# A weight-gradient matmul on one core: the accumulation order after slice 12 rearranged into whole phases, with the narrow part's banks taken in turn

## The chip, the cores and the metric

One core of one Trainium2 chip. The metric is the device time of the kernel in microseconds. The span of a profiled execution, from its first to its last instruction, is 1.7 to 1.9 us shorter than its measured time.

## The reference

```python
batch, m, k, n = 16, 512, 1024, 768
# float32 inputs
grad_weight = np.einsum('bmk,bmn->kn', input, grad_output)   # (1024, 768), float32
```

The 16 x 512 rows are one contraction of 8192, cut in 64 slices of 128.

## The kernel before: the parts that matter

The loads round each slice of both inputs to bfloat16 on the way in (all but slice 0, which is loaded as float32 and rounded by VectorE and ScalarE). They all stand at the start of the program, in order of slices, for GpSimd. In the trace GpSimd issues them one after the other, most of them when an earlier one has landed, the last at 136.8 us. There are 42 buffers for each input.

```python
for s in range(1, S):                       # S = 64
    gt = xg.tile([P, N], bf16, name="gt")   # grad_output, 128 x 768
    xt = xg.tile([P, K], bf16, name="xt")   # input, 128 x 1024
    nc.gpsimd.dma_start(out=gt, in_=G[s * P : (s + 1) * P, :])
    nc.gpsimd.dma_start(out=xt, in_=X[s * P : (s + 1) * P, :])
```

A slice needs twelve matmuls of 512 columns: four of part A and four of part B (output columns 0 to 511, wide) and four of the narrow part N (output columns 512 to 767, computed transposed). A part occupies four PSUM banks while it is open. There are eight banks and three parts, so the parts must take turns. When a part closes, VectorE adds its four banks to a sum in SBUF, and a bank can be reopened when its add is done.

```python
ORDER = (
    "A1! N1 B2! N2 A2 N3! A3 B3 A4! B5 N5 B6! N7 A6 N8! A9! B10 N9 B12! N12! A12! "
    "B15 A15 AB16 A19! B19! N19! A22 B22 AB28 A31! B31! N31! A34 B34 AB47 A50! B50! N64!"
).split()
# "A19!": run part A up to, not including, slice 19, then close it.
# "AB28": A and B by turns, slice by slice, up to slice 28.

def one_slice(part, close):
    s = part.done
    part.done += 1
    opened = part.banks is None
    if opened:                                # all four banks at once
        names = [free.pop(0) for _ in part.groups]
        part.banks = [(name, psum.tile([P, NA], f32, name=name)) for name in names]
    for i, (group, (name, bank)) in enumerate(zip(part.groups, part.banks)):
        part.matmul(bank, *group, s, opened, close)
        if close:
            ...                               # add (or first copy) to the sum in SBUF
            free.append(name)
    ...                                       # when it closes: the part has no banks any more
# ... afterwards: A and B from slice 50 on, bank by bank, each added and stored
```

## Time and profile before

| | before |
|---|---|
| median of the first three runs | 176.81 us (176.78 to 177.07) |
| span of the profiled run | 175.2 us |
| matmuls / weight loads in the program | 808 / 808 |
| VectorE instructions | 88 |
| x tile of one slice lands every | 2.2 us |
| TensorE needs for one slice (12 matmuls) | 2.59 us |

The lines that carry the reading are in the prediction below. How to read them: in a timeline each line is a start, a length, the engine, the source line, the operation and a count. A bracket at its end tells how long the engine had been idle and what ended that. L123 and L130 are the matmuls of the wide and the narrow parts, L114 is the adds. After the change the same lines are L124, L131 and L115. Matmuls are pipelined and the printed length of one (0.38 us) overlaps the next one's, so pace and pauses are read from starts. Some traces lack one matmul record in 50. Such a gap is one matmul of 0.216 us wide and is no pause.

### The profile page before, as it was taken

The numbers are of one execution on the slowest core, as the hardware profiler recorded it, in microseconds if no ns is written. First come the engines' busy times: TensorE is split into PE (matmuls) and PEld (weight loads), VectorE is DVE, ScalarE is ACT, GpSimd is POOL, SyncE is SP. The second block draws the span as 40 slices with busy tenths as digits, with TensorE's granted clock in tenths as the row PEclk, the third lists the DMA queues.
The fourth block names the chain that finished last, engine by engine and source line by source line (L and its number), as shares of the span: only waits on it lengthen the run. The fifth ranks groups of instructions, "written<-read, shape, count | busy, mean of one in ns | idle before, by whom it ended". The sixth has DMA issues, their size and how long they took to land.

```text
span 175.2 us, 1984 instructions
## 1 busy us (share of the span) xinstructions
PE 170.2 (97%) x793; PEld 78.3 (45%) x808; DVE 53.4 (30%) x88; ACT 5.7 (3%) x10; POOL 66.9 (38%) x130
## 2 busy tenths in 40 slices
PE   8999999999899999999999999999999999999993
PEld 3444444444344444444444444444444444444463
DVE  0555582880374100280320000047000003932122
ACT  3440000000000000000000000000000000000000
POOL 7544434444444444444444444444364200000000
PEclk9999999999999999999999999999999999999999
DMA  5999999999999999999999999999999990085623
GB/s 177 219 209 208 208 208 208 209 208 208 208 210 206 208 208 210 208 208 209 208 208 209 208 211 205 209 208 208 208 208 209 208 186 4 0 184 164 153 102 120
DMA packets 25192, 33.09 MB, mean 189 GB/s; under 512 B 6496, under 2 KB 16608, under 8 KB 25184
## 3 DMA queue, kind: packets, MB, share of 16 engines
q0 software_dynamic: 18144, 28.91, 90.3%
q1 hardware_dynamic: 2592, 2.49, 4.4%
q10 hardware_dynamic: 4448, 1.57, 3.9%
q8 instruction: 6, 0.10, 0.2%
q14 instruction: 2, 0.02, 0.0%
HBM read 58.72 MB, written 3.15 MB: 353 GB/s over the span
## 4 chain that ended last, share of the span: by engine, by line
PE 72%; DMA 24%; issue 1%; POOL 1%; DVE 0%; POOLq 0%
PE bank L123 46%; PE bank L130 26%; DMA xt<-in_input_dram 24%; POOL gt L92 1%; POOL xt L93 0%; DVE acc L114 0%; POOLq L228 0%
## 5 line engine op out<-in xcount | busy, mean ns | idle before, releaser
L123 PE MATMUL bank<-gt,xt 128*128 128x512 bf16 (+2 forms) x521 | 110.3, 368 | 1.2 <-DMA xt<-in_input_dram 0.6
L123 PEld LDWEIGHTS <-xt 128*128 128x128 bf16 x532 | 50.8, 98 | 59.2 <-DMA xt<-in_input_dram 1.4
L130 PE MATMUL bank<-xt,gt 128*128 128x512 bf16 x248 | 55.8, 379 | 0.2
L114 DVE TENSOR_TENSOR acc<-bank,acc 128x512 f32<-128x512 f32 (+2 forms) x54 | 33.1, 664 | 72.5 <-PE bank L123 71.9
L93 POOL DMA_DIRECT2D xt<-in_input_dram x63 | 33.5, 531 | 40.2 <-DMA xt<-in_input_dram 37.0
L92 POOL DMA_DIRECT2D gt<-in_grad_output_dram x63 | 33.5, 533 | 30.0 <-DMA gt<-in_grad_output_dram 28.5
L130 PEld LDWEIGHTS <-gt 128*128 128x128 bf16 x252 | 24.6, 98 | 29.8
L114 DVE TENSOR_TENSOR acct<-bank,acct 128x512 f32<-128x512 f32 x20 | 12.6, 679 | 39.4 <-PE bank L130 39.3
L80 PE MATMUL bank<-const-bfloat16-1.0 128*128 128x512 bf16 (+1 forms) x12 | 4.3, 547 | 0.8 <-PEq L228 0.8
L118 DVE COPY acc<-bank 128x512 f32<-128x512 f32 x4 | 2.7, 684 | 1.6 <-PE bank L123 1.5
L80 PEld LDWEIGHTS <-const-bfloat16-1.0 128*128 128x128 bf16 x12 | 1.6, 140 | 3.3 <-issue 3.3
L174 DVE STREAM_TRANSPOSE turned<-acct 128x512 f32<-128x512 f32 x4 | 2.9, 713 | 0.1
L123 PE MATMUL bank<-g,x 128*128 128x512 bf16 x8 | 2.7, 475 | 0.0
L120 ACT COPY acc<-bank 128x512 f32<-128x512 f32 x4 | 2.2, 587 | 1.8 <-PE bank L123 1.7
L105 DVE CAST g<-gf 128x256 bf16<-128x256 f32 x1 | 0.4, 440 | 4.2 <-DMA gf<-in_grad_output_dram 4.2
L118 DVE COPY acct<-bank 128x512 f32<-128x512 f32 x2 | 1.3, 686 | 1.3 <-PE bank L130 1.3
L106 ACT ACT_TABLE_LOAD x1 | 1.3, 1283 | 1.7 <-PEq L228 1.7
L123 PEld LDWEIGHTS <-x 128*128 128x128 bf16 x8 | 0.8, 114 | 1.1 <-issue 0.6
L120 ACT COPY acct<-bank 128x512 f32<-128x512 f32 x2 | 1.1, 588 | 1.5 <-PE bank L130 1.5
L130 PE MATMUL bank<-x,g 128*128 128x512 bf16 x4 | 1.0, 379 | 0.0
L106 ACT CAST x<-xf 128x256 bf16<-128x256 f32 x2 | 0.8, 402 | 0.5 <-DMA xf<-in_input_dram 0.5
L130 PEld LDWEIGHTS <-g 128*128 128x128 bf16 x4 | 0.4, 106 | 0.6 <-issue 0.3
(7 smaller groups left out, 1.7 us busy)
## 6 DMA issues: line engine op xcount, KB each, us to landing
xt<-in_input_dram POOLq DMA_DIRECT2D x63, 256.0 KB, 8.5
gt<-in_grad_output_dram POOLq DMA_DIRECT2D x63, 192.0 KB, 8.5
out_dram<-acc SPq DMA_DIRECT2D x13, 128.0 KB, 2.7
out_dram<-turned ACTq DMA_DIRECT2D x4, 256.0 KB, 3.2
xf<-in_input_dram ACTq DMA_DIRECT2D x2, 256.0 KB, 3.9
gf<-in_grad_output_dram SPq DMA_DIRECT2D x1, 256.0 KB, 3.5
out_dram<-acc SPq DMA_DIRECT2D x1, 256.0 KB, 2.0
gf<-in_grad_output_dram SPq DMA_DIRECT2D x1, 128.0 KB, 3.7
```

The lines of the kernel that those rows point to most:

```text
L80: nc.tensor.matmul(wps[:, 0:cols], ones, nc.const_aps.tensor(1.0, (P, cols), bf16), start=True, stop=True,)
L92: nc.gpsimd.dma_start(out=gt, in_=G[s * P : (s + 1) * P, :])
L93: nc.gpsimd.dma_start(out=xt, in_=X[s * P : (s + 1) * P, :])
L105: nc.vector.tensor_copy(out=dst[:, c : c + QX], in_=src[:, c : c + QX])
L106: nc.scalar.copy(out=dst[:, c + QX : c + 2 * QX], in_=src[:, c + QX : c + 2 * QX])
L114: nc.vector.tensor_add(out=dst, in0=src, in1=dst)
L118: nc.vector.tensor_copy(out=dst, in_=src)
L120: nc.scalar.copy(out=dst, in_=src)
L123: nc.tensor.matmul(bank, xs[s][:, k * P : (k + 1) * P], gwide[s][:, c0:c1], start=start, stop=stop)
L130: nc.tensor.matmul(bank, gnarrow[s].rearrange("p (r t) -> p t r", t=NT)[:, t], xs[s][:, h * NA : (h + 1) * NA], start=start, stop=stop,)
L174: nc.vector.transpose(out=turned[:, h * hb : (h + 1) * hb, :, t], in_=dst.rearrange("p (b r) -> p b r", r=SQ),)
```

## The change

Its intent: up to slice 12 nothing changes. After that A and B advance together through whole phases of 5, 9 and 15 slices, each followed by the narrow part over the same slices. The narrow part then takes its four banks one after the other (all slices of the phase into one bank, then the next), so that it needs a bank only when it comes to it. A small letter in the order stands for this.

```diff
-    "B15 A15 AB16 A19! B19! N19! A22 B22 AB28 A31! B31! N31! A34 B34 AB47 A50! B50! N64!"
+    "B15 AB17! n17! AB26! n26! AB41! n41! AB47 A50! B50! N64!"
...
+    def bank_by_bank(part, upto):
+        first = part.done
+        part.done = upto
+        for i in range(len(part.groups)):
+            open_bank(part, i)
+            for s in range(first, upto):
+                add_slice(part, i, s, s == first, s == upto - 1)
...
-        while any(parts[n].done < upto for n in names):
-            for n in names:
-                if parts[n].done < upto:
-                    one_slice(parts[n], close and parts[n].done == upto - 1)
+        if names.islower():
+            bank_by_bank(parts[names.upper()], upto)
+        else:
+            slice_by_slice(names, upto, close)
```

(The rest splits the old `one_slice` into `open_bank`, `add_slice` and `slice_by_slice`, which do for capital letters what it did.)

## The prediction

> **What bounds the kernel now.** I read the page first, then the list of waits, then the chain that ended last, and last the timelines of TensorE, VectorE and GpSimd around the one place where TensorE stood still. The page's first part and its strip of 40 slices:
>
> ```profile
> PE 170.2 (97%) x793; PEld 78.3 (45%) x808; DVE 53.4 (30%) x88; ACT 5.7 (3%) x10; POOL 66.9 (38%) x130
> ...
> PE   8999999999899999999999999999999999999993
> ...
> PEclk9999999999999999999999999999999999999999
> ```
>
> TensorE is busy from end to end at a full clock. The program has 808 matmuls (12 warm-up, 64 slices of 12, and 28 more because the last bank's 14 slices come in three pieces), and there are 808 weight loads but 793 matmul records: 15 are missing, so a busy share alone proves nothing. The pace has to come from starts. Timeline of TensorE, 20 to 56 us:
>
> ```profile
> 34.10 11.39 PE L123 MATMUL bank<-gt,xt 128*128 128x512 bf16 x51
> 46.07 3.63 PE L123 MATMUL bank<-gt,xt 128*128 128x512 bf16 x15 [0.58 <-DMA xt<-in_input_dram]
> 49.53 6.21 PE L130 MATMUL bank<-xt,gt 128*128 128x512 bf16 x28
> 55.58 0.59 PE L123 MATMUL bank<-gt,xt 128*128 128x512 bf16 x2
> ```
>
> The narrow part takes its slices 12 to 18 there, 7 x 4 = 28 matmuls, from 49.53 to 55.58: 6.05 / 28 = 0.216 us each. The stretch that begins at 34.10 holds 52 matmuls by the program (A of slices 9 to 11, B and A of 12 to 14, A and B of 15, A of 16 and 17; one record is missing). It should have ended at 34.10 + 52 x 0.216 = 45.33, and the next matmul, A of slice 18, started at 46.07. So TensorE really stood still 0.74 us (the 0.58 printed counts from a modelled end). The list of waits, its rows for TensorE and the weight loads that name a transfer or a bank:
>
> ```profile
> PEld L123 <- DMA xt<-in_input_dram: 1.4, 2, 1.1
> ...
> PE bank L123 <- DMA xt<-in_input_dram: 0.6, 1, 0.6
> ```
>
> No row has TensorE waiting for VectorE or ScalarE: banks are never late. The 1.1 is the weight load before this same matmul; the other weight-load gap, 0.3 us, moves no matmul start. The chain shows the same switch:
>
> ```profile
> 28.66 8.54 DMA xt<-in_input_dram
> 37.20 0.28 issue
> 37.48 8.54 DMA xt<-in_input_dram
> 46.02 0.05 issue
> 46.07 0.82 PE bank L123 x3
> ...
> 165.87 6.51 PE bank L123 x57
> 172.38 0.03 issue
> 172.40 0.29 DVE acc L114
> ```
>
> Up to 46 us the loads are on the chain, after it TensorE alone, with 0.05 us breaks that are the missing records. Slice 18's x tile landed at 46.02 and released its matmul 0.05 later. Slice 14's landed at 37.20, so a slice lands every (46.02 - 37.20) / 4 = 2.205 us, while TensorE needs 12 x 0.216 = 2.592 us for one. Loads are faster than TensorE, but the lead is small early on. The rest of the span is 4.91 us of start (first casts and warm-up) and about 3 us of the last add and store after the last matmul.
>
> **What the Trainium skill says.** "TensorE: Matmul & The Clock Gate", section "Wait — 56ns, not 53.3ns?", gives N / 2.4 GHz + about 2.5 ns between warm matmuls, 215.7 ns for 512 columns; the 0.216 us here agrees, so no order of matmuls can make one cheaper. "PSUM — Partial Sum Buffer", section "PSUM bank collisions raise a hardware error", wants a bank guarded against matmuls while another engine reads it; so a bank that is reopened must wait for its eviction, and each first matmul of a group in the changed order does wait on VectorE. "Perfetto Trace Analysis", section "Matmuls", wants independent groups to rotate through banks so that evictions overlap; both kernels do. "SBUF — State Buffer", section "Who interferes with whom", says that a VectorE instruction with at most one SBUF input outside the two-port modes does not contend with GpSimd, which matters because GpSimd makes the load descriptors. The adds read one bank and one SBUF tile. In this trace GpSimd issues x tiles at 46.31 and 48.52, during eight adds (46.50 to 51.57), and at 41.91 and 44.09 with VectorE idle: 2.21 against 2.18 us apart, so it agrees.
>
> **The change part by part.** The order up to slice 12, the start, the tail (A and B from slice 50, bank by bank) and all loads are untouched. Matmuls: the same 808, same shapes. Removed: the middle schedule, where A ran ahead to slice 18 alone. Added: A and B together to 17, narrow to 17; then to 26; then to 41; then as before. Closes of all three parts between 12 and 50/64 go from 9 to 12 groups of four, so 12 more adds.
>
> (a) *The 0.74 us wait.* Number the real matmuls from 0; slice 12 is complete at 144, B of 12 to 14 takes 144 to 155. A of slice 18 was number 184 at an unstalled 45.33. In the new order, "AB17" takes turns: A12, B15, A13, B16, A14, A15, A16. So B15 is number 160, at 45.33 - 24 x 0.216 = 40.15; its x tile landed at 46.02 - 3 x 2.205 = 39.41: 0.74 spare. B16 is number 168, at 41.87; slice 16 landed at 46.02 - 2 x 2.205 = 41.61: 0.26 spare, 0.21 after the 0.05 from landing to start. Number 184 is now the narrow part on slices 12 to 16, all there. No wait: **-0.74 us**.
>
> (b) *New waits for data?* The narrow part to 17 is 20 matmuls, so AB26 begins at 45.33 + 4.32 = 49.65. Each slice of AB takes 8 x 0.216 = 1.73 us against 2.205 between landings, so the lead shrinks by 0.48 a slice and is least at the last one. Slice 25: needed at 49.65 + 8 x 1.728 = 63.47, landed at 46.02 + 7 x 2.205 = 61.46, 2.0 spare. AB41 begins 108 matmuls after AB26, at 72.98; slice 40 is needed at 72.98 + 14 x 1.728 = 97.17 and lands at about 94.5, 2.6 spare. Slice 49 comes long after. The last: narrow on slice 63, number 652, at 45.33 + 468 x 0.216 = 146.42; by the last issue (136.8) plus 8.5 us to landing it lands at 145.3: 1.1 spare, where the kernel before had 1.84. **0**. The phases of 5, 9 and 15 look fitted to exactly these leads.
>
> (c) *New waits for banks?* An add starts 0.43 us after its group's last matmul starts (46.07 to 46.50), takes 0.69, and follows the next by about 0.60 (four in 2.48 us). Going into a narrow phase from slice 17 on, its first bank is the one A closed eight matmuls earlier: 8 x 0.216 - 0.43 - 0.69 = 0.61 us spare; into the first one it is B16's, closed long before. Within a phase a bank's turn lasts 5, 9 or 15 x 0.216 = 1.08, 1.94 or 3.24 us, longer than an add. Coming out, A takes banks evicted before, and B's fourth group takes the bank the narrow part closed last: 8 starts from that matmul to its reopening, again 0.61 spare. VectorE's queue must not be behind: in the shortest phase A's four adds run from 44.89, narrow adds follow at about 47.3, 47.9, 48.8 and 49.9, so the last is ready when its bank is. **0**.
>
> (d) *The 12 more adds*, 12 x 0.664 = 8.0 us by the row's mean, lie on an engine that is idle 70% of the span and end no wait. **0**.
>
> Sum: 176.81 - 0.74 = 176.07.
>
> **Rivals.** One: slice 16, with 0.2 us to spare, comes late. Landings slip in this very trace (slice 9's x tile landed 3.04 us after slice 8's). For it: a spare of 0.2 is smaller than such a slip. Against: a common lateness of all loads delays slice 11 first, which has no spare at all (B11 at 30.62 by the count, landed at 30.59), and so shifts TensorE as well. At worst it would take back what was gained: 176.3 to 176.8. Two: banks reopen late, because four narrow groups now close one by one among eight others. If all six phase edges lost 0.6 us by a slow release, 3.6 us would come to 179.7; the spare of 0.61 at each edge and the measured queue speak against. Three: consecutive matmuls into one bank run faster or slower than in rotation. The tail already does just that, at the same 10.79 us for 50, so 0 either way. Four: the extra adds hold up GpSimd and so loads; the issue distances above speak against it. Five: the tail or the stores hide the gain. TensorE alone is on the chain from 46 us to the last add, so 0.74 earlier there is 0.74 earlier at the end.
>
> **Range and chances.** The ceiling of the gain is the one wait, since nothing else on TensorE is idle: no less than about 176.0, with the run-to-run spread of 0.3 us below 175.8. Upward, rival one ends at 176.8. So 176.1, range 175.8 to 176.8. For 2% either way 3.5 us is needed: faster has nothing to come from (1 in 100), slower only by rival two or by something I don't see (2 in 100).
>
> **What would show it.** No gap in matmul starts at 45 to 47 us beyond one missing record; VectorE's count 100 in place of 88; narrow stretches of 20, 36 and 60 matmuls from about 45.3, 65.2 and 98.9 us; the last matmul 0.74 us earlier. Wrong if TensorE waits for slice 16 at 41.9, for slice 63 at 146, or if a wait for VectorE stands before a reopened bank.

## The result and the profile after

The changed kernel took 176.32 us (median of 4 runs, 176.06 to 176.42), the kernel before 176.89 us in the same set. The ratio is 0.9965, with a 95% interval of 0.9947 to 0.9982. A ratio here is the mean time of one kernel's fast runs over that of the other's of the same rounds, so it isn't quite the ratio of the medians quoted. Two more sets of runs gave 0.9954 and 0.9950 (below). So the gain is real and 0.35 to 0.5%, far under 2%.

The page of the changed kernel (busy time, share and count of each engine):

```profile
PE 170.8 (98%) x808; PEld 78.2 (45%) x808; DVE 60.8 (35%) x100; ACT 5.6 (3%) x10; POOL 66.9 (38%) x130
```

VectorE has 100 instructions where it had 88 and is busy 7.4 us longer. TensorE has the same work; this trace lost no record. The list of waits, limited to TensorE, has a single row, the one before the first warm-up matmul:

```profile
PE bank L81 <- PEq L252: 0.8, 1, 0.8
```

The row with 0.6 us for an x tile is gone. The timeline of TensorE shows the place itself:

```profile
34.20 11.39 PE L124 MATMUL bank<-gt,xt 128*128 128x512 bf16 x52
45.42 4.48 PE L131 MATMUL bank<-xt,gt 128*128 128x512 bf16 x20
49.74 15.70 PE L124 MATMUL bank<-gt,xt 128*128 128x512 bf16 x72
65.28 7.93 PE L131 MATMUL bank<-xt,gt 128*128 128x512 bf16 x36
```

The reader can check each start from the line above it: 34.20 + 52 x 0.216 = 45.43, then + 20 x 0.216 = 49.75, then + 72 x 0.216 = 65.3. There is no pause. The chain that ended last now runs without a load in it from 8.15 us to the end; its first and last pieces after that load are:

```profile
8.11 0.05 issue
8.15 1.04 PE bank L124 x4
...
147.46 24.26 PE bank L124 x140
171.71 0.02 issue
171.74 0.29 DVE acc L115
```

Before, the last add of the chain stood at 172.40; here at 171.74, 0.66 us earlier. That is the 0.74 us of the wait less about 0.1 us, and the 0.1 is seen in the first line of each timeline: the stretch that began at 34.10 before begins at 34.20 here, because slices 1 and 11 landed 0.24 and 0.10 us later in this execution. TensorE stood still 0.28 us for slice 1 and 0.12 us for slice 11 in this profile. Both are too short to be a row of that list. The order up to slice 12 is the same in both kernels, so slice 11 can hold up either of them: in the profile of the kernel before it cost 0.04 us. (The prediction has that this gap "moves no matmul start"; it moved them by those 0.04 us.)

The adds of the first new phase, in the timeline of VectorE:

```profile
42.38 5.08 DVE L115 TENSOR_TENSOR acc<-bank,acc 128x512 f32<-128x512 f32 x8 [3.56 <-PE bank L124]
47.37 1.28 DVE L115 TENSOR_TENSOR acct<-bank,acct 128x512 f32<-128x512 f32 x2
48.86 0.69 DVE L115 TENSOR_TENSOR acct<-bank,acct 128x512 f32<-128x512 f32 x1 [0.20 <-PE bank L131]
49.94 0.69 DVE L115 TENSOR_TENSOR acct<-bank,acct 128x512 f32<-128x512 f32 x1 [0.39 <-PE bank L131]
```

Four narrow banks end one by one, and their adds start at 47.37, 47.97 (the second of the x2), 48.86 and 49.94. The prediction had counted 47.3, 47.9, 48.8 and 49.9.

### The profile page after: what moved, and what is told of

Its sections match the earlier page's. It is cut to its first block, busy times and chain, and to the rows that moved or that the text cites. A ratio compares the mean times of both kernels' runs of the same rounds, so it can differ in the third digit from the quotient of the medians.

```text
span 174.5 us, 2024 instructions
## 1 busy us (share of the span) xinstructions
PE 170.8 (98%) x808; PEld 78.2 (45%) x808; DVE 60.8 (35%) x100; ACT 5.6 (3%) x10; POOL 66.9 (38%) x130
## 4 chain that ended last, share of the span: by engine, by line
PE 94%; DMA 4%; issue 0%; POOL 0%; DVE 0%; POOLq 0%
PE bank L124 63%; PE bank L131 31%; DMA xt<-in_input_dram 4%; POOL gt L93 0%; DVE acc L115 0%; POOLq L252 0%
## 5 line engine op out<-in xcount | busy, mean ns | idle before, releaser
L115 DVE TENSOR_TENSOR acc<-bank,acc 128x512 f32<-128x512 f32 (+2 forms) x62 | 37.9, 667 | 73.5 <-PE bank L124 73.1
L115 DVE TENSOR_TENSOR acct<-bank,acct 128x512 f32<-128x512 f32 x24 | 15.7, 682 | 30.0 <-PE bank L131 29.9
L106 DVE CAST x<-xf 128x256 bf16<-128x256 f32 x2 | 0.6, 287 | 0.3 <-DMA xf<-in_input_dram 0.3
```

What stands on the lines that cost most here:

```text
L106: nc.vector.tensor_copy(out=dst[:, c : c + QX], in_=src[:, c : c + QX])
L115: nc.vector.tensor_add(out=dst, in0=src, in1=dst)
```

## The experiments

The theory under test: the change removed one wait of 0.74 us for slice 18's data, and everything else in it costs and gains nothing. The rivals: whole phases or banks taken in turn make TensorE faster by themselves; the 12 more adds cost something; the small spares of the new schedule don't matter; and, the other way, the banks in turn don't matter either. There were seven runs of six kernels, in two sets with the kernel before in each (experiments 1 to 4 on one chip, 5 to 7 on another), and all gave correct results.

### 1. The change once more

No edit.

> The changed kernel once more, so that the others share a chip with it. Theory (the change removed one wait of 0.74 us for slice 18's data and cost nothing): 0.5 to 0.8 us under the kernel before of the same rounds. Rival (the difference on record was run-to-run spread, which is 0.3 us): anywhere from 0 to 0.3 us under it.

Measured: 176.12 us (5 runs), the kernel before 176.99 us (9 runs), ratio 0.9954, interval 0.9942 to 0.9967. By the medians 0.87 us, a little over the 0.5 to 0.8 expected. It isn't spread alone: no run of this set overlaps (176.30 is the slowest of one, 176.74 the fastest of the other).

### 2. Only the wait removed, in the old structure

```diff
-    "B15 A15 AB16 A19! B19! N19! A22 B22 AB28 A31! B31! N31! A34 B34 AB47 A50! B50! N64!"
+    "B15 A15 AB16 A18! B18! N18! A22 B22 AB28 A30! B30! N30! A34 B34 AB47 A50! B50! N64!"
```

> The kernel before, with its rotating narrow part, and only the two numbers changed that let A run ahead: to slices 18 and 30 in place of 19 and 31. Counted as in the prediction at 0.216 us a matmul: A of slice 18 is not needed until long after it landed, slice 29 just in time (under 0.1 us of wait), so TensorE loses 0.74 us less. Theory (the wait for data is all there is to the change): 0.6 to 0.75 us under the kernel before, level with the changed kernel within 0.2 us, with 88 VectorE instructions. Rival (taking narrow banks in turn or the whole phases make TensorE faster by themselves): near the kernel before, at least 0.3 us over the changed kernel. Second rival (the 12 more adds of the change cost something): under the changed kernel by more than 0.2 us.

Measured: 176.23 us, 0.76 us under the kernel before (0.6 to 0.75 expected), ratio to before 0.9963 (0.9950 to 0.9975), level with the changed kernel of the same set (0.9954) within 0.2 us. Its VectorE has 88 instructions. Its TensorE timeline:

```profile
34.27 13.11 PE L123 MATMUL bank<-gt,xt 128*128 128x512 bf16 x58
47.22 5.34 PE L130 MATMUL bank<-xt,gt 128*128 128x512 bf16 x24
```

By the order the first line holds 60 matmuls (A of 9 to 11, B and A of 12 to 14, A and B of 15, A of 16 and 17, B of 16 and 17; two records are missing), and 34.27 + 60 x 0.216 = 47.23. There is no pause. What follows: two changed numbers, without phases and without banks in turn, bring the whole gain. So neither of those makes TensorE faster, and the 12 adds that this kernel doesn't have cost the changed kernel nothing that these runs resolve. Slice 29, which the expectation had as just in time, had 0.28 us to spare (landed at 70.25, first used at 70.53). But TensorE lost 0.18 us for slice 49 (a gap of 0.393 us between starts in place of 0.216), which the expectation did not name. It is first used by matmul 504, at 45.33 + 320 x 0.216 = 114.45 by the count, and landed at 114.69 in this profile, which was taken of the slowest of the five runs (176.55): this order has no spare there. The changed one uses slice 49 only at 123.98, and it landed at 114.99. Since this kernel has a loss of its own, its time alone would not show a cost of the adds of up to 0.2 us; that they cost nothing is read from the changed kernel's timeline too, which has no pause after slice 11.

### 3. The wait put back, in the new structure

```diff
-    "B15 AB17! n17! AB26! n26! AB41! n41! AB47 A50! B50! N64!"
+    "B15 AB19! n19! AB26! n26! AB41! n41! AB47 A50! B50! N64!"
```

> The changed kernel with its first whole phase ending at slice 19 in place of 17. Theory: B of slice 17 is matmul 176, at 43.6 us, lands 43.8; B of slice 18 is matmul 184, lands 46.0; two waits of about 0.25 and 0.5 us, 0.74 in sum, so the time goes back to that of the kernel before (within 0.2 us) while the phases and the banks in turn stay. Rival (phases or banks in turn are what helped): stays within 0.3 us of the changed kernel.

Measured: 176.92 us, ratio to the kernel before 0.9997 (0.9985 to 1.0010). The timeline of TensorE:

```profile
34.08 11.67 PE L124 MATMUL bank<-gt,xt 128*128 128x512 bf16 x51
46.08 3.63 PE L124 MATMUL bank<-gt,xt 128*128 128x512 bf16 x15 [0.33 <-DMA xt<-in_input_dram]
49.55 6.21 PE L131 MATMUL bank<-xt,gt 128*128 128x512 bf16 x28
```

The stretch from 34.08 to slice 18 holds 52 matmuls, one record missing, and ends 0.77 us late: 46.08 - 34.08 - 52 x 0.216. By starts it is two gaps, 0.27 us for slice 17 and 0.50 us for slice 18; the first is hidden inside the line's 11.67, since the view joins what is less than 0.15 us apart by modelled ends. The narrow stretch then starts at 49.55, where the kernel before had 49.53. So the whole gain goes when the first phase is two slices longer, phases and banks in turn notwithstanding. That the wait alone decides, within the 0.2 us that these runs resolve, is shown from both sides.

### 4. The narrow part's banks all at once

```diff
-    "B15 AB17! n17! AB26! n26! AB41! n41! AB47 A50! B50! N64!"
+    "B15 AB17! N17! AB26! N26! AB41! N41! AB47 A50! B50! N64!"
```

> The changed kernel with the same phases, but the narrow part of phases 17, 26 and 41 again slice by slice over four banks at once. Theory (banks in turn are there because A and B now close together): the third and fourth bank of a part are reopened 10 and 11 matmuls after A0's last, 2.16 and 2.38 us, while their evictions end 0.43 + 2 or 3 x 0.60 + 0.69 = 2.3 and 2.9 us after it; about 0.24 and 0.38 us of wait at each of five phase edges, 3.1 us in sum, so about 179.4 us, and TensorE rows that wait for VectorE. Rival (VectorE's queue has room enough, banks in turn change nothing): within 0.3 us of the changed kernel and no wait for VectorE.

Measured: 179.02 us, ratio to the kernel before 1.0120 (1.0104 to 1.0135), 2.9 us over the changed kernel of the same set (3.1 expected). The list of waits, limited to TensorE, has rows that no other kernel here has:

```profile
PE bank L124 <- DVE acct L115: 0.7, 3, 0.2
PE bank L131 <- DVE acc L115: 0.4, 2, 0.2
```

Five waits for VectorE, at the five edges counted. (A third row, 0.2 us for an x tile, is slice 11's, before the part that was changed.) The printed 0.2 us each are the last of two at each edge and count from a modelled end; by starts each edge has a gap of about 0.20 us and one of about 0.38 us over the 0.216 of a matmul, 0.58 in sum and 2.9 us for five. The expectation's 0.24 us does not follow from the figures beside it: 0.43 + 2 x 0.60 + 0.69 - 2.16 is 0.16, and with 0.38 that makes 2.7 us for five. The waits came out between the two sums. TensorE and VectorE at the first edge:

```profile
49.51 1.87 PE L124 MATMUL bank<-gt,xt 128*128 128x512 bf16 x7
51.60 14.19 PE L124 MATMUL bank<-gt,xt 128*128 128x512 bf16 x64 [0.22 <-DVE acct L115]
```

```profile
49.06 2.48 DVE L115 TENSOR_TENSOR acct<-bank,acct 128x512 f32<-128x512 f32 x4 [1.83 <-PE bank L131]
```

Four banks that close 0.216 us apart are added 0.60 us apart. The last add ends at 49.06 + 2.48 = 51.54, and the matmul that reopens that bank starts at 51.60; without a wait it would have been at 49.51 + 7 x 0.216 = 51.02. So banks in turn add no speed, but they are what makes it possible for A and B to close together: without them the same phases lose over three times what the removed wait gave.

### 5. Phases too long for the lead

```diff
-    "B15 AB17! n17! AB26! n26! AB41! n41! AB47 A50! B50! N64!"
+    "B15 AB17! n17! AB33! n33! AB47 A50! B50! N64!"
```

> The changed kernel with phases 9 and 15 made one phase of 16 slices, 17 to 32, then straight on to the phase that ends at 50: as many groups as in the kernel before. Theory: the lead shrinks by 2.205 - 1.728 = 0.48 us a slice; slice 25 has 2.0 to spare, so slice 29 has about 0.1 and slices 30, 31 and 32 make TensorE wait about 0.48 each, 1.4 to 1.5 us in sum; 1.3 to 1.6 us over the changed kernel, nothing for VectorE. Rival (a spare of 0.2 us or more matters little because loads catch up): under 0.7 us over it.

Measured: 177.88 us, the changed kernel in the same set 176.20 us, so 1.68 us more, a little over the 1.3 to 1.6 expected (ratios to the kernel before 1.0045 and 0.9950). The timeline of TensorE:

```profile
72.85 1.90 PE L124 MATMUL bank<-gt,xt 128*128 128x512 bf16 x8 [0.34 <-DMA xt<-in_input_dram]
75.01 1.90 PE L124 MATMUL bank<-gt,xt 128*128 128x512 bf16 x8 [0.26 <-DMA xt<-in_input_dram]
77.27 1.90 PE L124 MATMUL bank<-gt,xt 128*128 128x512 bf16 x8 [0.36 <-DMA xt<-in_input_dram]
79.01 11.17 PE L131 MATMUL bank<-xt,gt 128*128 128x512 bf16 x51
```

At slices 30, 31 and 32, eight matmuls each, TensorE waits for each x tile, at the three slices counted. The lines start 2.16 and 2.26 us apart, which is the loads' pace of 2.2 and not TensorE's 1.73. By starts the three pauses are 0.51, 0.43 and 0.52 us, 1.45 in sum, as counted (1.4 to 1.5). For the rest of the 1.68, 0.2 us, the profiles show one place: slice 11 landed at 30.84 us here and at 30.64 in the changed kernel's profile of the same set (experiment 7), and from there on TensorE of both has no other pause in which to make it up. That this holds for all the runs behind the medians is not shown. The number of groups is that of the kernel before and VectorE has 88 instructions, so it isn't the groups that made the difference.

### 6. Slice 11 needed later

```diff
-    ... A9! B10 N9 B12! N12! A12! "
+    ... A9! B10 N10 B12! N12! A12! "
```

> The changed kernel with one narrow slice moved ahead of two of B (N10 in place of N9), so that slices 10 and 11 are needed four matmuls, 0.86 us, later. In the changed kernel's profiled run slice 11 cost 0.12 us and slice 1 cost 0.28. Theory: 0 to 0.15 us under the changed kernel, not to be told from it by time, and no gap in TensorE's starts around 30 us. Rival (the places of little spare early on cost more in most runs than in the profiled one): 0.3 us or more under it.

Measured: 176.09 us (6 runs, 175.86 to 177.31), ratio to before 0.9957 (0.9931 to 0.9983), against 176.20 us and 0.9950 for the changed kernel in the same set. By time the two can't be told apart. The timeline of TensorE shows that no pause is left:

```profile
28.88 1.89 PE L131 MATMUL bank<-xt,gt 128*128 128x512 bf16 x8
30.61 1.89 PE L124 MATMUL bank<-gt,xt 128*128 128x512 bf16 x8
32.33 1.89 PE L131 MATMUL bank<-xt,gt 128*128 128x512 bf16 x8
34.06 11.39 PE L124 MATMUL bank<-gt,xt 128*128 128x512 bf16 x52
```

From 28.88 each stretch starts 8 x 0.216 = 1.73 us after the last. In this profile the starts show no gap between the first real matmul and the last (the first three come at the warm-up's slower pace, 0.43 us apart). Slice 1's pause is absent too, but not by the edit: its x tile landed at 7.83 us here and at 8.11 in the first profile of the changed kernel. The last begins at 171.34 us; in the three profiles of the changed kernel it begins at 171.33 to 171.48. So for this list of matmuls the middle of the kernel has nothing left to give: what remains lies in the first 5 us and the last 3.

### 7. The change beside 5 and 6

No edit.

> The changed kernel beside the two above on the same chip: 0.6 to 0.9 us under the kernel before, as in the first set (0.9954).

Measured: 176.20 us, ratio 0.9950 (0.9937 to 0.9963), 0.77 us by the medians, as expected. In its profile TensorE waited 0.57 us for slice 1, twice what the first profile shows, and yet the last matmul began at 171.44 us against 171.48 there. Slice 1 landed at 8.11 us in both, so the longer wait only says that TensorE came to it earlier.

## Why the prediction was right

- *The number.* 176.07 was counted from 176.81; measured were 176.32, 176.12 and 176.20, beside 176.89, 176.99 and 176.97 for the kernel before. The signs named came too: 100 VectorE instructions, no gap at 45 to 47 us, narrow stretches from 45.42, 65.28 and 98.94 us, the last matmul 0.66 us earlier.
- *The bound.* TensorE, one matmul every 0.216 us, with one pause. Right: the removal of the pause moved the end by itself (2), and its return undid the gain (3).
- *(a) The wait.* 0.74 us on the count; 0.66 us in the first pair of profiles, and 0.57, 0.87 and 0.77 us by the medians of the three sets. Right within the spread. The spare for slice 16, counted as 0.26 us from landing to matmul, was 0.24, 0.22 and 0.21 us in the three profiles of the changed kernel, and no wait came of it.
- *(b) No new waits for data.* Right, and the arithmetic of the lead (2.205 less 1.728 us a slice) was tested where it must fail: experiment 5 waits exactly at the slices counted. In the changed kernel's first profile one load (slice 20) slipped by 1.1 us near 51 us, and the same in its third; slices 25 and 40 still landed at 62.08 and 95.15, 1.5 and 2.1 us before they were needed. Slice 63 landed at 145.86 and was needed at 146.43: 0.57 us of spare in place of the 1.1 counted, and 0.47 in the third profile. The count was right that it suffices, but it holds for loads without a slip.
- *(c) No new waits for banks.* Right. The two figures behind it, 0.43 us from a matmul's start to its add and 0.60 us from add to add, were put to the test by experiment 4: they give 2.7 us (the expectation wrote 3.1), and it came to 2.9.
- *(d) The adds are free.* Right within 0.2 us: experiment 2 lacks them and is not faster.
- *Rivals.* One (slice 16 late) did not happen in any profile; it stays possible in principle, as loads slip now and then, but no run shows it. Two is what experiment 4 shows for the same phases without banks in turn. Three fell by the changed kernel's own starts: 20 matmuls with the banks in turn take 49.74 - 45.42 = 4.32 us, 0.216 each. Four was set aside in the prediction by the distance of two issues, but GpSimd's issues wait for landings there (0.70 to 0.74 us before each x tile), so their distance can't tell; that an issue takes 0.53 us with adds beside it and without is the better sign. Slice 63's x tile landed at 145.38 to 145.91 us in the changed kernel's profiles, at 145.32 before, and at 145.20 in experiment 4, which has the 12 more adds too: they don't hold up the loads as a rule. (The slip at slice 20 stands in two profiles of the changed kernel and in no other; its third profile and experiments 3, 4 and 6, with 12 more adds as well, are without it.) Five fell by the end of the chain.

What stays open: the difference between the three sets' gains (0.57 to 0.87 us) is not resolved further than to spread and to the landings of the first slices.

## What to carry to other kernels

When an engine is 97% busy, count from starts what it would do with no pause at all: that gives the whole possible gain (here 0.74 us) before any change is made. A schedule that lets several consumers run ahead of loads has a lead that shrinks at a known rate; phase lengths can be fitted to it with a few lines of arithmetic, and one slice too many shows as a wait of that size. A group that closes all its banks at once needs as many adds of time before they are reopened; where the schedule leaves none, take the banks one after another.

## What the Trainium skill lacked or had wrong

- "VectorE: DVE Perf Modes", section "The TRN2 errata", gives 120 + FD cycles for an instruction from PSUM to SBUF, 0.658 us for 512 elements. Adds of a bank to an SBUF sum (one input from each, for which the table has no column of its own) followed each other at 0.598 us here (from one start to the next, inside the 2.48 us that four take), while a single one was 0.69 us long. The page's other figure, (N + 151) / 0.96 for a float32 `tensor_tensor`, 0.691 us, agrees with the single length.
- "PSUM — Partial Sum Buffer": wants a bank guarded, but has no time for handing it over. Here an add began 0.43 us after the start of its group's last matmul, 0.379 of which the profile counts as the matmul's own, modelled, length; and a waiting matmul began 0.05 us after the end of the add in experiment 4.
- "Perfetto Trace Analysis" doesn't say that matmul records can be missing at a fixed distance: five of the nine profiles here lack 15 of 808, one in 50, each looking like a pause of 0.216 us.
- "DMA: Bandwidth & Descriptors" gives no figure for single landings that slip in a steady stream. Here the x tile of slice 9 came 2.85 to 3.23 us after slice 8's in every profile, where 2.2 is usual, and in eight of the nine one or two later slices slipped by 0.3 to 1.1 us. The places differ from run to run, but come from a short list: slice 20, 33 or 34, 45 and 58, each in two or three profiles, so 11 to 14 slices apart, counted on from slice 9. No run here explains it.
